# Activations copied by DMA and transposed through their float32r view, SSD and forget rows in other queues and buffers

## The chip, the cores and the metric

One Trainium2 chip, one of its cores. The metric is the time of one execution on the device in microseconds (us); lower is better. Six units of the core appear below: TensorE (PE, with its weight loads PEld), VectorE (DVE), ScalarE (ACT), GpSimd (POOL), SyncE (SP) and the 16 DMA engines.

## The reference

Three transformer blocks follow each other on x, 256 tokens by 1024 features, in float32. Block one has two layers of feed-forward, mixer, feed-forward and a gated embedding; block two a hybrid mixer and an expert layer (PEER); block three a forgetting mixer and a convolutional feed-forward. What the change touches:

```python
def swiglu(x, w_in, w_out):                        # four times in block one; D_FF = 2816
    gate, up = jnp.split(x @ w_in, 2, axis=-1)
    return (jax.nn.silu(gate) * up) @ w_out

# PEER, 16384 experts, per token the gates gc of its chosen experts
act = jnp.einsum('td,thkd->thk', xc, u)
hact = jax.nn.gelu(act, approximate=False) * gc
return jnp.einsum('thk,thkd->td', hact, jnp.take(v_tab, ec, axis=0))

# SSD, 32 heads: a cumulative sum over time enters each head's decay matrix
acum = jnp.cumsum(ac, axis=1)
lmat = jnp.exp(jnp.where(causal, acum[:, :, None] - acum[:, None, :], -jnp.inf))

# forgetting attention, 16 heads, in blocks of 128 queries
sc = q @ k.T * scale + cum[:, :, qs:qe, None] - cum[:, :, None, :qe]
p = jax.nn.softmax(jnp.where(allowed, sc, -jnp.inf), axis=-1)
```

## The kernel before

**Products.** The tokens are two row tiles t of 128. Weights come as 900 chunks of 128x1024 float32 (`chunk`, L120 to L130): SP issues the DMA into one of 5 `raw` buffers, ACT copies it to a float32r high part `wh` (L128), DVE subtracts for the low part `wl` (L129), 8 buffers each. Every product is three float32r matmuls, high by high, low by high and high by low: L177, L178 and L181 in `seg`, L874 to L876 in the forms with other operands.

**Transposes.** An activation must lie with its features on the partitions before it can be multiplied. `split_T` (L217 to L228) transposes 128x128 blocks on PE against an identity `ident` (L225), up to four into one PSUM tile `tp`, of which there are two; ACT copies the high part out (L227), DVE computes the low part (L228).

**Feed-forward** (`ffn`, L343 to L372). The 2816 hidden columns are taken in five chunks of 512 and one of 256. For each chunk and each t, PE accumulates gate and up, ACT applies Silu (L364), DVE multiplies into `hnat` (L366), and `split_T` (L369) transposes four blocks (two in the last chunk). The next chunk's matmuls are already in PE's queue around these transposes.

**PEER** (`peer`, from L1481). The activations of all 16384 experts are computed densely and stored to DRAM (`act_d`, L1507), as are the gates (`gate_d`). Then 32 chunks of 512 experts follow: `prepare` (L1650) loads `va` (L1658) and `vg` (L1660) in SP's queue, DVE multiplies them in place (L1661), `split_T` (L1662) transposes `va`, and the chunk is multiplied with its weights.

**SSD and forget rows.** The cumulative sums are stored to DRAM (`cum_d`, L1256; in block three L1097) and read back repeated on all partitions by `rows_bcast` (L456 to L459), in SP's queue. In the SSD mixer, `unit(g)` (L1269) reads `RA` and `RB` (the tile `sil`) of group g; POOL masks them (L1295), ACT forms the exponentials (L1302, L1303) and Silu (L1291), PE multiplies (L1307, L1308, L1315). In block three `prep` (L1128 to L1133) loads `fR`, POOL masks it (L1132), DVE adds it to the scores (L1137); `attention` (L888 to L936) does scores (L885), softmax and the transposes into `apT` (L916, L922), for units of heads that `skew` (L41) runs interleaved. MoBA attention in block two uses the same function.

**Order.** Each engine executes its own queue in order. The order is fixed when the program is built, by a scheduler that places instructions by its estimates; a wait at the head of a queue holds all that stands behind it.

Of the kernel before, what the change touches and what calls it, by code (L numbers as in the profile page):

```python
# [16 lines left out]
P = 128  # L17
# [22 lines left out]

def skew(units):  # L41

    live = []
    units = list(units)
    while units or live:
        if units:
            live.insert(0, units.pop(0))
        live = [u for u in live if next(u, "end") != "end"]
        yield
# [13 lines left out]
class Net:  # L63
# [17 lines left out]
    def consts(self):  # L81
        nc = self.nc
        self.ident = self.cp.tile([P, P], F32, name="ident")
        nc.gpsimd.memset(self.ident, 0.0)
        nc.gpsimd.affine_select(out=self.ident, in_=self.ident, compare_op=ALU.not_equal, fill=1.0,
                                base=0, pattern=[[-1, P]], channel_multiplier=1)
        self.triu = self.cp.tile([P, P], F32, name="triu")
        nc.gpsimd.memset(self.triu, 1.0)
        nc.gpsimd.affine_select(out=self.triu, in_=self.triu, compare_op=ALU.is_ge, fill=0.0,
                                base=0, pattern=[[1, P]], channel_multiplier=-1)  # L90
        self.ones = self.cp.tile([P, P], F32, name="ones")
        nc.gpsimd.memset(self.ones, 1.0)
        self.cmask = self.cp.tile([P, P], F32, name="cmask")
        nc.gpsimd.memset(self.cmask, 0.0)
        nc.gpsimd.affine_select(out=self.cmask, in_=self.cmask, compare_op=ALU.is_ge, fill=NEG,
                                base=0, pattern=[[-1, P]], channel_multiplier=1)
        self.neghalf = self.cp.tile([P, 16], F32, name="neghalf")
        nc.gpsimd.memset(self.neghalf, -0.5)
# [117 lines left out]

    def split_T(self, src, dst_h, dst_l):  # L217

        nc = self.nc
        nb = src.shape[1] // P  # L220
        for b0 in range(0, nb, 4):
            m = min(4, nb - b0)
            tp = self.tp()
            for b in range(m):
                nc.tensor.transpose(tp[:, b * P:(b + 1) * P], src[:, (b0 + b) * P:(b0 + b + 1) * P], self.ident)  # L225
            v = tp[:, :m * P].rearrange("p (b t) -> p b t", t=P)
            nc.scalar.activation(dst_h[:, b0:b0 + m, :], v, AF.Copy)  # L227
            nc.vector.tensor_sub(dst_l[:, b0:b0 + m, :], v, dst_h[:, b0:b0 + m, :].bitcast(F32))  # L228
# [109 lines left out]
    def ffn(self, x, g_pre, g_post, l, i):  # L338
# [11 lines left out]
        for wd in widths:  # L350
# [11 lines left out]
            for t in range(2):  # L362
                sil = self.work("sil", [P, 512])
                nc.scalar.activation(sil[:, :wd], acc[t][:, :wd], AF.Silu, scale=rs[t])  # L364
                h = self.work("hnat", [P, 512])
                nc.vector.scalar_tensor_tensor(h[:, :wd], acc[t][:, wd:2 * wd], rs[t], sil[:, :wd],  # L366
                                               op0=ALU.mult, op1=ALU.mult)
                b0, nb = c0 // P, wd // P
                self.split_T(h[:, :wd], hs[t][:, b0:b0 + nb, :], ls[t][:, b0:b0 + nb, :])  # L369
            c0 += wd  # L370
# [84 lines left out]

    def rows_bcast(self, out, rows):  # L456

        (sa, na), (sb, nb) = rows.ap
        self.nc.sync.dma_start(out, bass.AP(tensor=rows.tensor, offset=rows.offset, ap=[[0, P], [sa, na], [sb, nb]]))  # L459

# [427 lines left out]
    def attention(self, mp, qT, kT, v, hs, ls, logits, prep=None):  # L888
# [3 lines left out]
        def unit(t, b0):  # L892
# [22 lines left out]
            yield  # L915
            pT = mp.tile([P, nb, 2, t + 1, P], F32, tag="apT", bufs=2, name=f"apT{u}")  # L916
            flat = pT.rearrange("p b j k q -> p (b j k) q")
# [17 lines left out]

        return skew(unit(t, b0) for t in range(2) for b0 in range(0, 8, 4 >> t))  # L936

# [125 lines left out]
    def forget_mixer(self, x):  # L1063
# [5 lines left out]
        with pool("spill3", space=bass.MemoryType.DRAM) as dp:  # L1069
# [6 lines left out]
            with pool("fgt") as fp:  # L1076
# [46 lines left out]
                with pool("fattn", reuse_waits="tile") as mp, pool("fyT", reuse_waits="tile") as yp:  # L1123
# [4 lines left out]
                    def prep(t, b0, W):  # L1128
                        R = mp.tile([P, W, (t + 1) * P], F32, tag="fR", bufs=1, name=f"fR{t}_{b0}")
                        self.rows_bcast(R, cumd[2 * b0:2 * b0 + W, :(t + 1) * P])  # L1130
# [37 lines left out]
            with pool("merge", reuse_waits="tile") as mp:  # L1168
                hs, ls, lhy = self.xT_tiles("yaT", 10, pool=mp)
                for t in range(2):  # L1170
                    for y, c in yn[t]:
                        k = slice(c // P, (c + y.shape[1]) // P)
                        self.split_T(y, hs[t][:, k, :], ls[t][:, k, :])
                merge(1, accb)
# [65 lines left out]
    def ssd(self, lhs, h_all, l_all, cumd, mp):  # L1240
# [14 lines left out]
        nc.vector.tensor_tensor_scan(lp, self.ones[:32, :1].to_broadcast([32, N]), a, 0.0, ALU.mult, ALU.add)  # L1255
        nc.sync.dma_start(cumd, lp)  # L1256
        nat = mp.tile([P, 4, 32], F32, name="dt_acum")
# [11 lines left out]
        def unit(g):  # L1269
# [4 lines left out]
            for R, c in ((RA, 0), (RB, P)):  # L1274
                self.rows_bcast(R, cumd[4 * g:4 * g + 4, c:])
            w = self.weights("w_in_2", (0,), kbs, [(OX + 256 * g, 256), (OX + 2048 + P * g, P), (OX + 3072 + P * g, P)])
# [204 lines left out]
    def peer(self, x):  # L1481
# [5 lines left out]
        with self.tc.tile_pool(name="peer_d", bufs=1, space=bass.MemoryType.DRAM) as dp:  # L1487
# [3 lines left out]
            with self.tc.tile_pool(name="peer1", bufs=1) as mp:  # L1491
# [156 lines left out]
                with self.tc.tile_pool(name="peer2", bufs=1) as vp:  # L1648
# [3 lines left out]
                    def prepare(c):  # L1652
# [3 lines left out]
                        for t in range(2):  # L1656
# [4 lines left out]
                            nc.vector.tensor_mul(a, a, gt)  # L1661
                            self.split_T(a, h[:, :, t * P:(t + 1) * P], l[:, :, t * P:(t + 1) * P])  # L1662
                        return [lambda kb, t=t: (h[:, kb, t * P:(t + 1) * P], l[:, kb, t * P:(t + 1) * P])
# [93 lines left out]
```

## Time and profile before

| | |
|---|---|
| time, median of 3 runs | 2857.23 us (2855.98 to 2858.57) |
| profiled execution: its own time | 2861.38 us |
| its span from first to last instruction | 2859.7 us |
| TensorE busy | 2797.2 us (98%) |
| VectorE, ScalarE, GpSimd busy | 1857.2, 1624.1, 115.9 us |
| DMA | 601.31 MB, 210 GB/s in the mean |

A row of the timeline joins equal instructions that follow each other (x4); its second number is from the first's start to the last's end. TensorE's matmuls overlap, so that the time of one is read from the distance of their starts. A bracket tells how long the engine was idle before the row, and what released it.

### The profile page before, as it was taken

The page shows a single profiled execution, that of the slowest core. Times are in us where ns is not written, and L with a number is a line of the kernel's source. Part 1 is how long each engine was busy: PE and PEld are TensorE (multiplying, and loading weights), DVE is VectorE, ACT ScalarE, POOL GpSimd, SP SyncE. Part 2 cuts the span into 40 slices and gives each one's busy share as a digit, 9 for nine tenths or more (in the row PEclk, how much of TensorE's full clock was granted, in tenths as well). Part 3 has the DMA queues.
Part 4 walks back from the last instruction along what each step waited for, and adds up shares of the span by engine and source line. Part 5 has one row for each costly group of instructions (what it writes and reads, how often), then busy time and mean ns, then how long its engine had stood idle before and what let it go on. Part 6 is the DMA issues. An engine that isn't in the chain of part 4 may idle for free. (4 is left out here: it accounts for less than half of the span.)

```text
span 2859.7 us, 39692 instructions
## 1 busy us (share of the span) xinstructions
PE 2797.2 (98%) x14844; PEld 2369.0 (83%) x14844; DVE 1857.2 (65%) x2641; ACT 1624.1 (57%) x2356; POOL 115.9 (4%) x178
## 2 busy tenths in 40 slices
PE   8999999999989999999999999999999999999998
PEld 7887788888768878999779878888888888877997
DVE  5555654755566466776664999566666657776784
ACT  5446544644475456777565469684444448655653
POOL 0000000200010012100000000000000000000000
PEclk9999999999999999999999999999999999999999
DMA  7554555665536465665656668788777756565553
GB/s 251 189 204 159 189 191 182 232 209 189 209 105 217 166 219 190 196 223 192 221 184 208 212 217 264 243 257 311 268 271 267 269 178 225 178 237 189 195 178 125
DMA packets 221161, 601.31 MB, mean 210 GB/s; under 512 B 21172, under 2 KB 67044, under 8 KB 220456
## 3 DMA queue, kind: packets, MB, share of 16 engines
q1 hardware_dynamic: 220664, 597.72, 61.8%
q8 instruction: 116, 1.90, 0.3%
q10 hardware_dynamic: 272, 1.05, 0.1%
q14 instruction: 77, 0.63, 0.1%
q0 software_dynamic: 32, 0.02, 0.0%
HBM read 548.84 MB, written 49.86 MB: 209 GB/s over the span
## 5 line engine op out<-in xcount | busy, mean ns | idle before, releaser
L129 DVE TENSOR_TENSOR wl<-raw,wh 128x1024 fp32r<-128x1024 f32 x900 | 1079.1, 1221 | 578.5 <-ACT wh L128 551.2
L128 ACT ACTIVATE wh<-raw 128x1024 fp32r<-128x1024 f32 x900 | 926.9, 1055 | 706.6 <-PE acc L181 522.9
L177 PE MATMUL acc<-wh,xTh_h 128*128 128x512 f32 (+2 forms) x1552 | 591.4, 383 | 0.8 <-ACT act L1506 0.5
L178 PE MATMUL acc<-wl,xTh_h 128*128 128x512 f32 (+2 forms) x1552 | 585.4, 379 | 2.6 <-DVE wl L129 2.6
L181 PE MATMUL acc<-wh,xTl_l 128*128 128x512 f32 (+2 forms) x1552 | 462.2, 379 | 0.0
L178 PEld LDWEIGHTS acc<-wl,xTh_h 128*128 128x128 f32 x1552 | 293.4, 189 | 53.7 <-DVE wl L129 2.9
L177 PEld LDWEIGHTS acc<-wh,xTh_h 128*128 128x128 f32 x1552 | 293.4, 189 | 53.1 <-issue 1.0
L181 PEld LDWEIGHTS acc<-wh,xTl_l 128*128 128x128 f32 x1552 | 286.2, 189 | 54.0 <-issue 1.0
L874 PE MATMUL acc<-xTh_h,wh 128*128 128x256 f32 x832 | 237.9, 286 | 0.5 <-DVE big L1395 0.5
L876 PE MATMUL acc<-xTh_h,wl 128*128 128x256 f32 x832 | 237.3, 285 | 0.0
L875 PE MATMUL acc<-xTl_l,wh 128*128 128x256 f32 x832 | 236.8, 285 | 0.0
L177 PE MATMUL acc<-wh,ehT 128*128 128x512 f32 x512 | 202.2, 395 | 0.4 <-ACT ehT L227 0.4
L178 PE MATMUL acc<-wl,ehT 128*128 128x512 f32 x512 | 199.5, 390 | 0.0
L874 PEld LDWEIGHTS acc<-xTh_h,wh 128*128 128x128 f32 x832 | 160.4, 193 | 0.9 <-ACT wh L128 0.7
L876 PEld LDWEIGHTS acc<-xTh_h,wl 128*128 128x128 f32 x832 | 160.5, 193 | 0.2
L875 PEld LDWEIGHTS acc<-xTl_l,wh 128*128 128x128 f32 x832 | 160.4, 193 | 0.2
L178 PE MATMUL acc<-wl,hTh_h 128*128 128x512 f32 x352 | 137.6, 391 | 0.0
L177 PE MATMUL acc<-wh,hTh_h 128*128 128x512 f32 x352 | 137.6, 391 | 0.0
L181 PE MATMUL acc<-wh,elT 128*128 128x512 f32 x512 | 137.0, 389 | 0.0
L204 POOL TENSOR_SCALAR s<-s 128x1 f32<-128x1 f32 (+3 forms) x66 | 30.6, 463 | 2287.0 <-ACT junk L214 2024.1
L181 PEld LDWEIGHTS acc<-wh,elT 128*128 128x128 f32 x512 | 96.1, 188 | 20.0
L177 PEld LDWEIGHTS acc<-wh,ehT 128*128 128x128 f32 x512 | 96.2, 188 | 19.5 <-ACT ehT L227 0.6
(483 smaller groups left out, 4203.9 us busy)
## 6 DMA issues: line engine op xcount, KB each, us to landing
raw<-in_w_dram SPq DMA_DIRECT2D x900, 512.0 KB, 4.8
act_d<-act SPq DMA_DIRECT2D x64, 256.0 KB, 3.6
gate_d<-gst SPq DMA_DIRECT2D x32, 512.0 KB, 5.0
va<-act_d SPq DMA_DIRECT2D x64, 256.0 KB, 5.2
vg<-gate_d SPq DMA_DIRECT2D x64, 256.0 KB, 5.1
gain<-in_norm_g_dram SPq DMA_DIRECT2D x18, 512.0 KB, 5.7
RA<-cum_d SPq DMA_DIRECT2D x8, 512.0 KB, 4.8
sg_d<-big SPq DMA_DIRECT2D x8, 512.0 KB, 5.8
```

What stands on the lines that cost most here:

```text
L128: nc.scalar.activation(hi, raw, AF.Copy)
L129: nc.vector.tensor_sub(lo, raw, hi.bitcast(F32))
L177: nc.tensor.matmul(o, xh, wh[:, s], start=first and i == 0, stop=False)
L178: nc.tensor.matmul(o, xh, wl[:, s], start=False, stop=False)
L181: nc.tensor.matmul(o, lhs[t](kbs[i])[1], w[i][0][:, s], start=False, stop=last and i == end)
L204: nc.gpsimd.tensor_scalar(m, ss, c / n, c * EPS, op0=ALU.mult, op1=ALU.add)
L874: nc.tensor.matmul(o, wh[:, s], xh, start=i == 0, stop=False)
L875: nc.tensor.matmul(o, wh[:, s], xl, start=False, stop=False)
L876: nc.tensor.matmul(o, wl[:, s], xh, start=False, stop=i == len(kbs) - 1)
```

## The change

An identity of type float32r, `identr`, takes the place of the float32 one, which becomes its view. A new function `loaded` copies an activation within on-chip memory by a DMA in GpSimd's queue, into one of two buffers, and `split_T` can transpose such a tile through float32r views of it, of the identity and of the PSUM tile. The feed-forward's `hnat` (48 copies, 176 transposes) and PEER's product (64 copies, 256 transposes) are copied and transposed so; the tiles `yn` of block three, which a DMA has loaded already, are transposed so without a copy (20 transposes). The other 658 transposes stay float32. In the SSD mixer the store of `cum_d` and the rows of group 0 go to GpSimd's queue. `fR` has two buffers instead of one, `apT` one instead of two, and the attention's units are advanced eldest first.

```diff
@@ -38,13 +38,14 @@
         return self.got[t]
 
 
-def skew(units):
+def skew(units, eldest=False):
+
 
     live = []
     units = list(units)
     while units or live:
         if units:
-            live.insert(0, units.pop(0))
+            live.insert(len(live) if eldest else 0, units.pop(0))
         live = [u for u in live if next(u, "end") != "end"]
         yield
 
@@ -80,11 +81,13 @@
 
     def consts(self):
         nc = self.nc
-        self.ident = self.cp.tile([P, P], F32, name="ident")
-        nc.gpsimd.memset(self.ident, 0.0)
-        nc.gpsimd.affine_select(out=self.ident, in_=self.ident, compare_op=ALU.not_equal, fill=1.0,
+        self.identr = self.cp.tile([P, P], F32R, name="identr")
+        self.ident = self.identr.bitcast(F32)
+        self.triu = self.cp.tile([P, P], F32, name="triu")
+        nc.gpsimd.memset(self.triu, 0.0)
+        nc.gpsimd.affine_select(out=self.triu, in_=self.triu, compare_op=ALU.not_equal, fill=1.0,
                                 base=0, pattern=[[-1, P]], channel_multiplier=1)
-        self.triu = self.cp.tile([P, P], F32, name="triu")
+        nc.scalar.activation(self.identr, self.triu, AF.Copy)
         nc.gpsimd.memset(self.triu, 1.0)
         nc.gpsimd.affine_select(out=self.triu, in_=self.triu, compare_op=ALU.is_ge, fill=0.0,
                                 base=0, pattern=[[1, P]], channel_multiplier=-1)
@@ -214,7 +217,14 @@
         nc.scalar.activation(junk[:, :n], src, AF.Square, scale=scale, accum_out=ss)
         return ss
 
-    def split_T(self, src, dst_h, dst_l):
+    def loaded(self, src, pool, tag, bufs=2):
+
+        self.n_small += 1
+        c = pool.tile(list(src.shape), F32, tag=tag, bufs=bufs, name=f"{tag}_{self.n_small}")
+        self.nc.gpsimd.dma_start(c, src)
+        return c
+
+    def split_T(self, src, dst_h, dst_l, loaded=False):
 
         nc = self.nc
         nb = src.shape[1] // P
@@ -222,7 +232,11 @@
             m = min(4, nb - b0)
             tp = self.tp()
             for b in range(m):
-                nc.tensor.transpose(tp[:, b * P:(b + 1) * P], src[:, (b0 + b) * P:(b0 + b + 1) * P], self.ident)
+                o, i = tp[:, b * P:(b + 1) * P], src[:, (b0 + b) * P:(b0 + b + 1) * P]
+                if loaded:
+                    nc.tensor.transpose(o.bitcast(F32R), i.bitcast(F32R), self.identr)
+                else:
+                    nc.tensor.transpose(o, i, self.ident)
             v = tp[:, :m * P].rearrange("p (b t) -> p b t", t=P)
             nc.scalar.activation(dst_h[:, b0:b0 + m, :], v, AF.Copy)
             nc.vector.tensor_sub(dst_l[:, b0:b0 + m, :], v, dst_h[:, b0:b0 + m, :].bitcast(F32))
@@ -366,7 +380,8 @@
                 nc.vector.scalar_tensor_tensor(h[:, :wd], acc[t][:, wd:2 * wd], rs[t], sil[:, :wd],
                                                op0=ALU.mult, op1=ALU.mult)
                 b0, nb = c0 // P, wd // P
-                self.split_T(h[:, :wd], hs[t][:, b0:b0 + nb, :], ls[t][:, b0:b0 + nb, :])
+                c = self.loaded(h[:, :wd], fp, f"hcopy{wd}")
+                self.split_T(c, hs[t][:, b0:b0 + nb, :], ls[t][:, b0:b0 + nb, :], True)
             c0 += wd
         acc = self.gemm_wide(hl, DFF // P, "w_ffn_out", (l, i))
         fctx.close()
@@ -453,10 +468,10 @@
 
         self.nc.tensor.transpose(out, col.to_broadcast([P, P]), self.ident)
 
-    def rows_bcast(self, out, rows):
+    def rows_bcast(self, out, rows, queue=None):
 
         (sa, na), (sb, nb) = rows.ap
-        self.nc.sync.dma_start(out, bass.AP(tensor=rows.tensor, offset=rows.offset, ap=[[0, P], [sa, na], [sb, nb]]))
+        (queue or self.nc.sync).dma_start(out, bass.AP(tensor=rows.tensor, offset=rows.offset, ap=[[0, P], [sa, na], [sb, nb]]))
 
     def transposes(self, dst, src, nb, engine="act"):
 
@@ -913,7 +928,7 @@
                 e = sm[:, c * half:(c + 1) * half, :]
                 nc.vector.tensor_mul(e, e, ri[:, c * half:(c + 1) * half, None].to_broadcast([P, half, nk]))
             yield
-            pT = mp.tile([P, nb, 2, t + 1, P], F32, tag="apT", bufs=2, name=f"apT{u}")
+            pT = mp.tile([P, nb, 2, t + 1, P], F32, tag="apT", bufs=1, name=f"apT{u}")
             flat = pT.rearrange("p b j k q -> p (b j k) q")
             for c in range(2):
                 tp = self.tp([P, 4, P])
@@ -933,7 +948,7 @@
             nc.scalar.activation(hs[t][:, b, :], o, AF.Copy)
             nc.vector.tensor_sub(ls[t][:, b, :], o, hs[t][:, b, :].bitcast(F32))
 
-        return skew(unit(t, b0) for t in range(2) for b0 in range(0, 8, 4 >> t))
+        return skew((unit(t, b0) for t in range(2) for b0 in range(0, 8, 4 >> t)), True)
 
     def rg_lru(self, lhs, ga, ya, mp):
 
@@ -1126,7 +1141,7 @@
                     hs, ls, lhy = self.xT_tiles("yT", KB, pool=yp)
 
                     def prep(t, b0, W):
-                        R = mp.tile([P, W, (t + 1) * P], F32, tag="fR", bufs=1, name=f"fR{t}_{b0}")
+                        R = mp.tile([P, W, (t + 1) * P], F32, tag="fR", bufs=2, name=f"fR{t}_{b0}")
                         self.rows_bcast(R, cumd[2 * b0:2 * b0 + W, :(t + 1) * P])
                         diag = R[:, :, t * P:]
                         nc.gpsimd.affine_select(out=diag, in_=diag, compare_op=ALU.is_ge, fill=-NEG, base=0,
@@ -1170,7 +1185,7 @@
                 for t in range(2):
                     for y, c in yn[t]:
                         k = slice(c // P, (c + y.shape[1]) // P)
-                        self.split_T(y, hs[t][:, k, :], ls[t][:, k, :])
+                        self.split_T(y, hs[t][:, k, :], ls[t][:, k, :], True)
                 merge(1, accb)
                 acca = self.gemm_wide(lhy, 10, "w_proj_a_3", (0,))
                 mh, ml, lhm = self.xT_tiles("mT", KB, pool=mp)
@@ -1253,7 +1268,7 @@
         nc.vector.scalar_tensor_tensor(f, f, 0.0, lp, op0=ALU.max, op1=ALU.add)
         nc.vector.tensor_scalar(a, f, ea, None, op0=ALU.mult)
         nc.vector.tensor_tensor_scan(lp, self.ones[:32, :1].to_broadcast([32, N]), a, 0.0, ALU.mult, ALU.add)
-        nc.sync.dma_start(cumd, lp)
+        nc.gpsimd.dma_start(cumd, lp)
         nat = mp.tile([P, 4, 32], F32, name="dt_acum")
         neg = mp.tile([P, 2, 32], F32, name="nacum")
         dt, acum, nacum = [nat[:, t, :] for t in range(2)], [nat[:, 2 + t, :] for t in range(2)], [neg[:, t, :] for t in range(2)]
@@ -1272,7 +1287,7 @@
             RB = self.work("sil", [P, 512]).rearrange("p (h t) -> p h t", h=4)
 
             for R, c in ((RA, 0), (RB, P)):
-                self.rows_bcast(R, cumd[4 * g:4 * g + 4, c:])
+                self.rows_bcast(R, cumd[4 * g:4 * g + 4, c:], None if g else nc.gpsimd)
             w = self.weights("w_in_2", (0,), kbs, [(OX + 256 * g, 256), (OX + 2048 + P * g, P), (OX + 3072 + P * g, P)])
             acc = self.acc2([P, 4, N])
             self.segT(lhs[2], kbs, w, [acc[:, n, :] for n in range(4)])
@@ -1659,7 +1674,8 @@
                             gt = vp.tile([P, 512], F32, tag="vg", bufs=4, name=f"vg{c}{t}")
                             nc.sync.dma_start(gt, gdv[t, :, e])
                             nc.vector.tensor_mul(a, a, gt)
-                            self.split_T(a, h[:, :, t * P:(t + 1) * P], l[:, :, t * P:(t + 1) * P])
+                            a = self.loaded(a, vp, "vc")
+                            self.split_T(a, h[:, :, t * P:(t + 1) * P], l[:, :, t * P:(t + 1) * P], True)
                         return [lambda kb, t=t: (h[:, kb, t * P:(t + 1) * P], l[:, kb, t * P:(t + 1) * P])
                                 for t in range(2)]
 
```

PE's queue at the border of two feed-forward chunks, before. `hnat_478` is t=0, `hnat_489` is t=1; `acc_37` belongs to the next chunk.

```order
L181 MATMUL acc_30_331<-wh_424,xTl_l_110 128x512 x2
L225 MATMUL tp_480<-ident,hnat_478 128x128 x4
L177 MATMUL acc_37_498<-wh_502,xTh_h_109 128x512
L178 MATMUL acc_37_498<-wl_503,xTh_h_109 128x512
L177 MATMUL acc_37_498<-wh_502,xTh_h_109 128x512
L178 MATMUL acc_37_498<-wl_503,xTh_h_109 128x512
L181 MATMUL acc_37_498<-wh_502,xTl_l_110 128x512 x2
L225 MATMUL tp_491<-ident,hnat_489 128x128 x4
L177 MATMUL acc_37_498<-wh_508,xTh_h_109 128x512
```

After, the same border; `hcopy_35` and `hcopy_39` are the copies for t=0 and t=1. First the transposes of t=0 and what follows them:

```order
L184 MATMUL acc_32_336<-wh_429,xTl_l_111 128x512 x2
L237 MATMUL tp_487<-identr,hcopy_35_485 128x128 x4
L180 MATMUL acc_41_507<-wh_511,xTh_h_110 128x512
L181 MATMUL acc_41_507<-wl_512,xTh_h_110 128x512
L180 MATMUL acc_41_507<-wh_511,xTh_h_110 128x512
L181 MATMUL acc_41_507<-wl_512,xTh_h_110 128x512
L184 MATMUL acc_41_507<-wh_511,xTl_l_111 128x512 x2
```

They are where they were. Six rows further on in PE's queue stands this, with the transposes of t=1 (`tp_500`):

```order
L181 MATMUL acc_41_507<-wl_524,xTh_h_110 128x512
L180 MATMUL acc_41_507<-wh_523,xTh_h_110 128x512
L181 MATMUL acc_41_507<-wl_524,xTh_h_110 128x512
L184 MATMUL acc_41_507<-wh_523,xTl_l_111 128x512 x2
L237 MATMUL tp_500<-identr,hcopy_39_498 128x128 x4
L180 MATMUL acc_41_507<-wh_529,xTh_h_110 128x512
L181 MATMUL acc_41_507<-wl_530,xTh_h_110 128x512
```

The transposes of t=0 stay at the border. Those of t=1 stood 6 matmuls behind them and now stand 18 behind, after the matmuls of three weight tiles (`wh_511`, `wh_517`, `wh_523`) instead of one.

SP's queue at the store of the SSD mixer's cumulative sum, before.

```order
L125 DMA raw_9144<-in_w_dram 128x1024
L1256 DMA cum_d<-hnat_8738 32x256
L459 DMA RA_8757<-cum_d 128x1024
L459 DMA sil_8758<-cum_d 128x4x128
L459 DMA RA_9128<-cum_d 128x1024
L459 DMA sil_9129<-cum_d 128x4x128
L125 DMA raw_9150<-in_w_dram 128x1024
L125 DMA raw_9270<-in_w_dram 128x1024
```

After, SP's queue at that place.

```order
L128 DMA raw_9235<-in_w_dram 128x1024
L128 DMA raw_9241<-in_w_dram 128x1024
L474 DMA RA_9225<-cum_d 128x1024
L128 DMA raw_9247<-in_w_dram 128x1024
L474 DMA sil_9226<-cum_d 128x4x128
L128 DMA raw_9367<-in_w_dram 128x1024
L128 DMA raw_9373<-in_w_dram 128x1024
```

The store and the first group's two rows are no longer there; the second group's stand between weights. GpSimd's queue at that place, after:

```order
L1271 DMA cum_d<-hnat_8835 32x256
L474 DMA RA_8854<-cum_d 128x1024
L474 DMA sil_8855<-cum_d 128x4x128
L1310 AFFINE_SELECT RA_9225<-RA_9225 128x4x128
L1310 AFFINE_SELECT RA_8854<-RA_8854 128x4x128
L1310 AFFINE_SELECT sil_8855<-sil_8855 128x512
L1310 AFFINE_SELECT sil_9226<-sil_9226 128x512
```

The store and the rows of the first group (`RA_8854`, `sil_8855`) stand here now, ahead of the masks.

SP's queue in the forgetting attention, before.

```order
L125 DMA raw_22313<-in_w_dram 128x1024
L459 DMA fR_0_21771<-cum_d 128x8x128
L1060 DMA sg_d<-big_21814 128x2x512
L125 DMA raw_22319<-in_w_dram 128x1024
L125 DMA raw_22325<-in_w_dram 128x1024
L125 DMA raw_22417<-in_w_dram 128x1024
L1119 DMA sil_22519<-ya_d 128x256
L459 DMA fR_4_21864<-cum_d 128x8x128
```

The two loads of `fR` are six rows apart. The same place, after:

```order
L128 DMA raw_22538<-in_w_dram 128x1024
L474 DMA fR_0_21996<-cum_d 128x8x128
L474 DMA fR_4_22102<-cum_d 128x8x128
L1075 DMA sg_d<-big_22039 128x2x512
L128 DMA raw_22544<-in_w_dram 128x1024
L128 DMA raw_22550<-in_w_dram 128x1024
L128 DMA raw_22642<-in_w_dram 128x1024
L474 DMA fR_0_22243<-cum_d 128x1024
```

The second load of `fR` now stands directly behind the first.

## Rows read from the trace of the kernel before

**Rows 1.** The page's first part: busy us (share) and instructions of each engine.
```profile
PE 2797.2 (98%) x14844; PEld 2369.0 (83%) x14844; DVE 1857.2 (65%) x2641; ACT 1624.1 (57%) x2356; POOL 115.9 (4%) x178
```

**Rows 2.** Waits of PE, whole span: line, releaser, total us, times, longest us.
```profile
PE tp L1315 <- ACT big L1404: 5.9, 2, 3.8
...
PE acc L1307 <- ACT ssdu L1291: 2.1, 1, 2.1
...
PE tp L225 <- DVE hnat L366: 1.3, 1, 1.3
```

**Rows 3.** Timeline at a feed-forward border: start, us, engine, line, operation [idle before].
```profile
77.85 0.75 DVE L366 SCALAR_TENSOR_TENSOR hnat<-acc,s,sil 128x512 f32<-128x512 f32 x1 [3.84 <-ACT sil L364]
...
82.37 0.60 PE L225 MATMUL tp<-ident,hnat 128*128 128x128 f32 x4
...
83.44 0.74 DVE L366 SCALAR_TENSOR_TENSOR hnat<-acc,s,sil 128x512 f32<-128x512 f32 x1
...
84.25 0.66 PE L225 MATMUL tp<-ident,hnat 128*128 128x128 f32 x4
```

**Rows 4.** Windows: PE, PEld, DVE, ACT, POOL busy, PEclk, DMA share, GB/s.
```profile
78.00:79.00 1.00, 1.00 (x6) 0.81 (x6) 0.60 (x1) 0.51 (x1) 0.00 (x0) 1.00 0.00 0
84.00:89.00 5.00, 5.00 (x25) 4.04 (x24) 2.55 (x4) 1.29 (x2) 0.00 (x0) 1.00 0.86 300
1138.00:1143.00 5.00, 5.00 (x31) 5.00 (x32) 2.38 (x3) 5.00 (x12) 3.10 (x2) 0.68 0.28 108
1960.00:2320.00 360.00, 359.65 (x1717) 300.36 (x1715) 223.33 (x246) 153.37 (x186) 0.00 (x0) 1.00 0.77 264
2520.00:2525.00 5.00, 5.00 (x19) 3.52 (x16) 3.55 (x4) 3.34 (x7) 0.98 (x1) 0.66 0.77 234
```

**Rows 5.** Source view of L225: engine, tiles, count, ns min/median/max, first and last start.
```profile
L225 PE MATMUL tp<-ident,va x256: 270/272/273, 1959.7 to 2315.3; 128*128 128x128 f32 x128
...
L225 PE MATMUL tp<-ident,hnat x176: 270/272/331, 35.4 to 986.5; 128*128 128x128 f32 x176
```

**Rows 6.** Timeline in the PEER stage at 1959 us.
```profile
1959.74 1.03 PE L225 MATMUL tp<-ident,va 128*128 128x128 f32 x8
```

**Rows 7.** Timeline of PE from 1142 to 1146 us.
```profile
1142.02 0.28 PE L876 MATMUL acc<-xTh_h,wl 128*128 128x256 f32 x1
...
1145.98 0.28 PE L876 MATMUL acc<-xTh_h,wl 128*128 128x256 f32 x1
```

**Rows 8.** Timeline in the PEER stage, 2013 to 2034 us.
```profile
2013.84 1.07 PE L181 MATMUL acc<-wh,elT 128*128 128x512 f32 x4
...
2014.79 0.69 DVE L1661 TENSOR_TENSOR va<-va,vg 128x512 f32<-128x512 f32 x1 [0.89 <-DMA va<-act_d]
...
2031.96 1.03 PE L225 MATMUL tp<-ident,va 128*128 128x128 f32 x8
```

**Rows 9.** Timeline around GpSimd's `cum_d` in the third block.
```profile
2372.38 0.68 DVE L1096 TENSOR_TENSOR_SCAN hnat<-ones,hnat 16x256 f32<-16x256 f32 x1
...
2373.36 0.71 POOL L1097 DMA_DIRECT2D cum_d<-hnat  x1 [28.91 <-DVE hnat L1096]
```

**Rows 10.** DMA view, 2370 to 2376 us: issues, KB each, median us to landing.
```profile
cum_d<-hnat POOLq DMA_DIRECT2D x1, 16.0 KB, 1.9
```

**Rows 11.** The page's sixth part: DMA issues, KB each, median us to landing.
```profile
act_d<-act SPq DMA_DIRECT2D x64, 256.0 KB, 3.6
```

**Rows 12.** Timeline around the SSD rows, SP's queue and ACT.
```profile
1118.30 3.13 SPq L125 DMA_DIRECT2D raw<-in_w_dram  x4
...
1126.23 1.06 ACT L128 ACTIVATE wh<-raw 128x1024 fp32r<-128x1024 f32 x1 [6.78 <-DMA raw<-in_w_dram]
```

**Rows 13.** Waits from 2495 to 2575 us.
```profile
POOL fR L1132 <- DMA fR<-cum_d: 26.1, 4, 7.4
...
DVE asm L1137 <- POOL fR L1132: 9.2, 6, 4.9
...
PE acc L885 <- DVE asm L1137: 3.4, 2, 2.1
```

## The prediction

> **What bounds the kernel now.** I read the page first: TensorE is busy 2797.2 of 2859.7 us, 98% [rows 1]. So only two things can move the time: how long TensorE's own instructions are, and the few places where it waits. The list of what TensorE waits for comes second; its waits are small and each stands at one place: 5.9 us in the SSD mixer (two waits for ScalarE's `big`, L1404), 2.1 us there for `ssdu` (L1291), and 1.3 us in one wait for `hnat` [rows 2]. The third view is the timeline where the change adds a wait, at the border of two column chunks of a feed-forward layer [rows 3]. The fourth is a table of windows, because the new copies go through the same DMA engines as the weights: these engines stand still at 78 to 79 us and are 86% busy from 84 to 89 us [rows 4].
>
> **The float32r view of 452 transposes.** 44 transposes in each of four feed-forward layers (176), 256 in PEER and 20 of `yn` in the third block change their type; 176 and 256 are the counts of the rows of L225 [rows 5]. Matmuls are pipelined, so their median of 272 ns is not what one costs. Eight transposes in one row take 1.03 us; without the last one's 0.27 that is 0.76 over seven steps, 0.109 us each [rows 6]. A float32r instruction with 128 columns is not in this trace. Those with 256 columns follow each other every 0.12 us (from 1142.02 to 1145.98, 33 steps) [rows 7], and those with 512 every 0.227 (four in 1.07 us, the last 0.39 of it: 0.68 / 3) [rows 8]. The straight line through both is 0.107 us for 256 columns and 0.013 besides, so 0.066 for 128. That is the low end. The high end is 0.120, if 128 columns cost what 256 do. I take 0.075, near the line, a little above it because the weights of a transpose are loaded for it alone and nothing wider hides that. 452 × (0.109 − 0.075) = **−15.4 us**; ends −19.4 and +5. It counts in full, since TensorE has no slack in these stages: from 1960 to 2320 us it is busy 359.65 of 360 us [rows 4].
>
> **The 48 feed-forward copies.** Before, TensorE transposes what VectorE has just written. At this border the second half (t=1) is ready at 83.44 + 0.74 = 84.18 and transposed from 84.25: a slack of 0.07 us. The first half (t=0) is ready at 77.85 + 0.75 = 78.60 and transposed at 82.37: 3.77 us [rows 3]. Now a copy by DMA stands between. The new order gives the t=1 transposes 12 more float32r matmuls of 0.227 us before them (11 in the first and the last chunk of a layer), while the t=0 transposes ahead of them are 4 × 0.034 us shorter: 0.07 + 12 × 0.227 − 0.14 = 2.65, or 2.43 with 11. Sixteen and eight of these make a mean slack of 2.57 us, in 24 places.
>
> How long is it from `hnat` to the landed copy? The nearest row is the only transfer that GpSimd issues after a VectorE result: the scan ends at 2372.38 + 0.68 = 2373.06, GpSimd issues at 2373.36 (0.30 later), and its 16 KB land 1.9 us after issue [rows 9, 10]. The copy is 256 KB, about 245 KB more. From 1960 to 2320 us the engines move 264 GB/s at a share of 0.77, so 343 at full share [rows 4]: 0.72 us more alone, 1.43 at half rate beside weights. So 0.30 + 1.9 + 0.72 = 2.9 us or 3.6. The t=0 copy falls into the stretch without DMA traffic [rows 4], and 2.9 us are covered by 3.77 us of matmuls. The t=1 copy, from 84.5 us on, falls into weight traffic at a share of 0.86: 0.86 × 1.43 + 0.14 × 0.72 = 1.33, so 3.5 us. The same 256 KB in SP's queue, `act_d`, take 3.6 us from issue [rows 11], but some of that is weights ahead of them in that queue, and a part of the 1.9 is already the transfer of the 16 KB. I take 3.4 us. TensorE then waits 3.4 − 2.57 = 0.83 us 24 times, as nothing else can run ahead of the transposes in its queue: **+20 us**. Ends: 2.9 us gives +8, 3.6 us +25; without end at the bottom a copy in 2.57 us gives 0.
>
> The Trainium skill ("DMA: Bandwidth & Descriptors", section "Anatomy of one DMA — SWDGE (gpsimd) path") puts a transfer of this kind at about 2.0 us and its bytes over 436 GB/s, 2.6 us here as an estimate; with the sum otherwise as it stands, this term would be about +1 in place of +20. The same page ("Queues, rings and completion order") says that each DMA engine takes turns between queues packet by packet, which speaks for half the rate beside weights. No transfer of 256 KB by GpSimd is in this trace, so neither is shown.
>
> **The 64 PEER copies.** The product of a chunk is done at 2014.79 + 0.69 = 2015.48 and its transposes start at 2031.96 [rows 8]: 16.5 us for a copy of 3.5. Two `vc` buffers allow a copy to start only when the chunk before is transposed, about 11 us ahead (356 us for 32 chunks [rows 5]); that still covers it. They add 16.8 MB to a stage whose DMA share is 0.77 [rows 4]; 16.8 MB over 360 us are 47 GB/s, a share of 0.14 more, so 0.91. **0**; if weights then come late I would expect +5.
>
> **SSD rows in other queues.** SP issues `cum_d` and four loads of its rows (1.5 MB) before the next weights, which it issues at 1118.30. ScalarE is idle 6.78 us, until 1126.23, for these weights [rows 12]. This delay comes back to TensorE as the 2.1 and 5.9 us of L1307 and L1315 [rows 2], and behind the second wait the granted clock is 0.68 of full from 1138 to 1143 (a part of these 5 us at 1.2 GHz, the rest at 2.4) [rows 4], 1.6 us lost. Now half of the rows stand in GpSimd's queue, and SP goes on with weights. Their bytes still share the engines, so half of the 6.78 us is saved at best: **−3 us**; ends 0 and −9.6, all three.
>
> **Forget rows, two buffers.** With one `fR`, the next load waits until the masked scores are read; GpSimd waits 26.1 us for these loads and TensorE 3.4 us in two pieces for what follows [rows 13], with 0.66 clock from 2520 to 2525 (1.7 us lost) [rows 4]. Now two loads stand back to back in SP's queue. −3.5 of the possible −5.1; on the other side, one `apT` instead of two and the order that begins with the eldest unit may cost 2: ends −5.1 and +2. The MoBA attention uses the same order; I give it 0 (±2), and the start, where `identr` takes one more ScalarE step, 0.
>
> **Sum.** −15.4 + 20 − 3 − 3.5 = −1.9 on the profiled execution's 2861.38: 2859.5. That execution is 4.15 above the median of 2857.23, so by the median **2855 us**. Without the copies' term the sum is −21.9, so the whole question is the landing time: at 3.48 us the change is worth nothing; under 3.24 it is faster by over 0.2% (5.7 us, about what a measurement of this kernel can tell from no change), over 3.72 slower by as much.
>
> **The rivals.** *The copies land in time.* If a landing takes 2.6 us, the t=1 term is 24 × 0.03, and the sum is −21: 2836. For it: the 1.9 us row is a write to DRAM of small packets, and a copy within SBUF may be quicker. Against it: 0.30 and 1.9 alone are 2.2, and 245 KB must pass in 0.4 us, at over 600 GB/s, more than any window here moves. The skill's 2.6 us gives the same time.
>
> *The copies are later than I think.* If weights go first at each engine and the copy gets a third of the rate, its transfer is 2.15 us and the landing 4.35: a wait of 1.78 × 24 = 43, sum +21, 2878. It decides from 3.72 us on. The granted clock fell behind the longest wait of the forget rows, 2.1 us [rows 4, 13]; should it fall behind these waits, they cost more. For it: `act_d`'s 3.6 us [rows 11]. Against it: at 84 to 89 us the engines have a seventh of their time free.
>
> *The view gains nothing.* If a 128-column transpose keeps its 0.109 us in either type, only +20 − 6.5 is left: 2871. For it: 256-column instructions take 0.12, so a floor per instruction can't be excluded. Against it: f32 transposes take twice what the line gives. The Trainium skill ("TensorE: Matmul & The Clock Gate", section "Terms") says that the transpose mode of this chip is four times faster for FP32; by that rule the f32 transposes are in the fast form already and this rival holds.
>
> **How the numbers follow.** Forecast, late by 0.3 to 1.2 us: 0.45, its own range 2841 to 2866; within it about 0.17 faster, 0.18 same, 0.10 slower. In time: 0.28, all faster. Later: 0.15, all slower. No gain: 0.12, of which 0.02 still within the bound. Together 0.45 faster, 0.20 same, 0.35 slower. The range runs from 2830 (in time with 0.066 us a transpose is 2832; only larger gains at the SSD and forget rows lie lower) to 2879 (the third-rate case).
>
> **What would show it.** The float32r transposes of `vc` in steps of 0.075 us (0.066 to 0.109): eight in about 0.8 us. TensorE's wait for DMA `hcopy` at t=1, 24 times, some 20 us in all; none at t=0; the DMA list's landing of `hcopy512` about 3.1 us from issue. The waits of L1307, L1315 and the scores' matmuls together some 6 us shorter. The prediction fails if t=0 copies are waited for too, if PEER's transposes wait for `vc`, or if weights come late in the PEER stage.

## The result: 2.6% slower

The changed kernel takes 2934.4 us (median of 4 runs, 2927.7 to 2935.4) against 2856.9 for the kernel before: a ratio of 1.0264, 95% interval 1.0252 to 1.0277. The forecast of 2855 was wrong, and so was its range. The profiled execution of the changed kernel took 2935.37 us, with a span of 2933.6.

The page of the changed kernel, part one, and two of its DMA issues (KB each, median us to landing), answer to [rows 1, 11]:

```profile
PE 2816.5 (96%) x14844; PEld 2375.3 (81%) x14844; DVE 1853.3 (63%) x2641; ACT 1624.4 (55%) x2357; POOL 178.4 (6%) x293
...
vc<-va POOLq DMA_DIRECT2D x64, 256.0 KB, 3.9
hcopy<-hnat POOLq DMA_DIRECT2D x40, 256.0 KB, 3.3
```

TensorE has as many instructions as before, is busy 19 us longer and idle 55 us longer. Its waits (total us, times, longest), beside [rows 2, 13]:

```profile
PE tp L237 <- DMA hcopy<-hnat: 56.9, 24, 3.6
...
PE tp L1330 <- ACT big L1419: 4.2, 2, 2.9
PE tp L237 <- DMA vc<-va: 2.8, 1, 2.8
...
PE acc L900 <- DVE asm L1152: 1.7, 1, 1.7
...
PE acc L1322 <- ACT ssdu L1306: 0.3, 1, 0.3
```

One new wait accounts for nearly all of the added idle time. It stands 24 times, as the prediction said, but lasts 2.37 us and not 0.83. The waits of L1307, L1315 and L885 (now L1322, L1330 and L900) are together 6.2 us instead of 11.4: 5.2 less, where the prediction had some 6.

The four feed-forward layers, from the same TensorE instruction to the same one, in windows (PE, PEld, DVE, ACT, POOL busy; granted clock; DMA share; GB/s). First of the kernel before, then of the changed kernel:

```profile
8.30:188.40 180.10, 178.28 (x800) 146.60 (x801) 99.99 (x97) 88.28 (x99) 0.97 (x3) 1.00 0.61 210
337.80:492.30 154.50, 154.47 (x702) 126.97 (x701) 82.87 (x81) 71.84 (x80) 0.00 (x0) 1.00 0.56 190
601.30:755.70 154.40, 154.40 (x701) 127.00 (x701) 81.84 (x80) 70.90 (x79) 0.00 (x0) 1.00 0.57 196
866.60:1020.20 153.60, 153.60 (x703) 126.44 (x701) 78.85 (x78) 70.33 (x80) 0.22 (x1) 1.00 0.55 188
sum 642.60, PE 640.75 PEld 527.01 DVE 343.55 ACT 301.35 POOL 1.18; mean PE 160.19 PEld 131.75 DVE 85.89 ACT 75.34 POOL 0.30
```

```profile
7.90:207.10 199.20, 183.66 (x801) 149.21 (x802) 100.43 (x97) 88.27 (x99) 8.84 (x17) 0.97 0.59 206
356.40:531.80 175.40, 160.54 (x702) 130.89 (x701) 83.48 (x81) 71.99 (x81) 5.90 (x11) 0.96 0.53 182
640.80:815.00 174.20, 160.87 (x702) 130.91 (x701) 82.54 (x80) 70.85 (x79) 5.90 (x11) 0.96 0.55 187
925.30:1101.30 176.00, 161.70 (x703) 131.52 (x702) 79.32 (x78) 70.35 (x80) 6.76 (x13) 0.95 0.52 180
sum 724.80, PE 666.78 PEld 542.52 DVE 345.76 ACT 301.47 POOL 27.41; mean PE 166.69 PEld 135.63 DVE 86.44 ACT 75.37 POOL 6.85
```

They take 724.8 us instead of 642.6: 82.2 us more, and the whole span grew by 73.9. 56.2 of them are idle time (58.0 against 1.85). The other 26 are busy time, because the granted clock, 1.00 in all four windows before, is 0.95 to 0.97: (1 − clock) times the length is 29 us, and the faster transposes take 3 to 4 off that. The 29 us do not come from every border: by the records of the granted clock, 16 of the 24 waits are followed by a stretch at half the clock, 58 us in all, and eight are not. A wait of 2.5 us and the clock behind it, in three windows of the changed kernel:

```profile
60.00:69.50 9.50, 7.47 (x36) 5.82 (x34) 6.11 (x6) 4.25 (x5) 0.55 (x1) 1.00 0.77 263
69.50:76.30 6.80, 6.30 (x18) 5.07 (x19) 0.69 (x1) 0.89 (x2) 0.00 (x0) 0.50 0.06 23
76.30:85.00 8.70, 8.70 (x40) 7.21 (x39) 4.90 (x4) 3.96 (x4) 0.00 (x0) 1.00 0.55 180
```

The wait ends at 70.0. From 69.5 to 76.3 the granted clock is 0.50, the lower of the two levels (1.2 GHz): 18 matmuls in 6.30 busy us are 0.35 us each, the 40 in the next 8.70 are 0.22.

Now the border itself, which answers to [rows 3]. Timeline of the changed kernel; 87.51 is the copy for t=0, 93.10 that for t=1:

```profile
87.51 0.55 POOL L224 DMA_DIRECT2D hcopy<-hnat  x1 [22.03 <-DVE hnat L380]
...
90.98 0.46 PE L237 MATMUL tp<-identr,hcopy 128*128 128x128 f32 x4
...
92.06 0.75 DVE L380 SCALAR_TENSOR_TENSOR hnat<-acc,s,sil 128x512 f32<-128x512 f32 x1
...
93.10 0.55 POOL L224 DMA_DIRECT2D hcopy<-hnat  x1 [5.04 <-DVE hnat L380]
...
98.16 0.51 PE L237 MATMUL tp<-identr,hcopy 128*128 128x128 f32 x4 [2.55 <-DMA hcopy<-hnat]
```

`hnat` is ready at 92.81, GpSimd issues 0.29 us later, and TensorE would have been ready at 95.61: a slack of 2.8 us at this border, 2.65 by the prediction (over the 24 borders 2.77, where it had 2.57). What failed is the landing. The DMA view, from 87 to 91 us (the t=0 copy) and from 92 to 99 us (the t=1 copy):

```profile
hcopy<-hnat POOLq DMA_DIRECT2D x1, 256.0 KB, 2.2
```

```profile
hcopy<-hnat POOLq DMA_DIRECT2D x1, 256.0 KB, 4.9
```

The same copy of 256 KB takes 2.2 us on idle DMA engines and 4.9 beside weights. Over the 24 borders, four of which have copies of 128 KB, the first is 1.9 to 2.5, the second 4.1 to 5.4 us (mean 4.7). The DMA view in two windows after the t=1 issue, 93.1 to 95.4 and 95.4 to 97.8 us (queue: packets, MB, share of 16 engines; q1 is the weights, q0 the copy), shows how:

```profile
q1 hardware_dynamic: 196, 0.74, 86.7%
```

```profile
q1 hardware_dynamic: 171, 0.59, 63.3%
q0 software_dynamic: 80, 0.26, 26.9%
```

For 2.3 us no packet of the copy moves; then its 80 packets take 2.2 us, among packets of weights. Alone, at t=0, the first packet moves 1.1 us after issue and all of them within 0.9.

### The profile page after: what moved, and what is told of

It is laid out like the page before. It is cut to its first block, busy times and chain, and to the rows that moved or that the text cites. A ratio compares the mean times of both kernels' runs of the same rounds, so it can differ in the third digit from the quotient of the medians.

```text
span 2933.6 us, 40143 instructions
## 1 busy us (share of the span) xinstructions
PE 2816.5 (96%) x14844; PEld 2375.3 (81%) x14844; DVE 1853.3 (63%) x2641; ACT 1624.4 (55%) x2357; POOL 178.4 (6%) x293
## 4 chain that ended last, share of the span: by engine, by line
PE 66%; issue 16%; DVE 7%; DMA 5%; ACT 4%; POOL 2%; SPq 0%; DVEq 0%; POOLq 0%; ACTq 0%
PE acc L180 14%; PE acc L184 14%; PE acc L181 14%; PE acc L891 3%; PE acc L890 3%; PE acc L889 3%; DVE wl L132 2%; PE acc L342 2%; DMA hcopy<-hnat 2%; PE acc L343 2%; DMA raw<-in_w_dram 2%; PE acc L345 2%; ACT wh L131 1%; PE acc L1612 1%; PE tp L237 1%
## 5 line engine op out<-in xcount | busy, mean ns | idle before, releaser
L180 PE MATMUL acc<-wh,xTh_h 128*128 128x512 f32 (+2 forms) x1552 | 601.3, 390 | 0.8 <-ACT act L1521 0.5
L181 PE MATMUL acc<-wl,xTh_h 128*128 128x512 f32 (+2 forms) x1552 | 594.2, 385 | 2.5 <-DVE wl L132 2.5
L184 PE MATMUL acc<-wh,xTl_l 128*128 128x512 f32 (+2 forms) x1552 | 472.2, 386 | 0.0
L180 PEld LDWEIGHTS acc<-wh,xTh_h 128*128 128x128 f32 x1552 | 299.5, 193 | 55.8 <-issue 2.0
L181 PEld LDWEIGHTS acc<-wl,xTh_h 128*128 128x128 f32 x1552 | 299.5, 193 | 55.4 <-DVE wl L132 2.9
L1676 DVE TENSOR_TENSOR va<-va,vg 128x512 f32<-128x512 f32 x64 | 43.3, 692 | 139.2 <-DMA va<-act_d 128.1
L181 PEld LDWEIGHTS acc<-wl,ehT 128*128 128x128 f32 x512 | 96.8, 189 | 19.4
```

The source lines that it names most:

```text
L180: nc.tensor.matmul(o, xh, wh[:, s], start=first and i == 0, stop=False)
L181: nc.tensor.matmul(o, xh, wl[:, s], start=False, stop=False)
L184: nc.tensor.matmul(o, lhs[t](kbs[i])[1], w[i][0][:, s], start=False, stop=last and i == end)
```

## The experiments

Theory A: the loss is the t=1 copies, which stand behind weight packets on the DMA engines. Rivals: other edits lose too (B), the copies cost by their traffic (C), or GpSimd's path is slow at t=1 for another reason (D).

**Without the feed-forward copies** (`no_ffn_copy`).

```diff
-                c = self.loaded(h[:, :wd], fp, f"hcopy{wd}")
-                self.split_T(c, hs[t][:, b0:b0 + nb, :], ls[t][:, b0:b0 + nb, :], True)
+                self.split_T(h[:, :wd], hs[t][:, b0:b0 + nb, :], ls[t][:, b0:b0 + nb, :])
```

> The changed kernel without the 48 feed-forward copies (their 176 transposes are float32 again, straight from the product); all other edits stay. Theory A: the loss is made by the late t=1 copies alone (57 us of waits for them, some 26 us of low clock behind these waits, less 4 us that the faster transposes give), so without them 2934 falls by about 80 to 2851 us (2846 to 2856). Rival B: the float32r transposes, the PEER copies or the moved rows lose too; then the time stays above 2865 us.

2856.9 us against 2856.5 for the kernel before, ratio 1.0001 (0.9991 to 1.0010). The whole loss of 77.5 us is gone; B is out. But the time is above the expected band (2846 to 2856): the remaining edits together gain nothing that can be measured, not 5 us.

**The feed-forward copies alone** (`ffn_copies_only`): the kernel before with `loaded` in the feed-forward and nothing else of the change.

> The kernel before with the 48 feed-forward copies and their 176 float32r transposes, nothing else of the change. Theory A: the whole loss is here, 24 waits of about 2.4 us and the low clock behind them: 2934 us (2928 to 2940). If the copies lose only together with the other edits: under 2900 us.

2939.7 us in one run, with 56.3 us of waits in 24 places. The loss is complete without any other edit.

**A quiet DMA** (`quiet_weights`).

```diff
+        if not again:                       # again: w_ffn_in, three of four chunks
+            self.raw = self.wp.tile([P, CH], F32, tag="raw", bufs=RAWB, name=f"raw{i}")
+            nc.sync.dma_start(self.raw, self.d["w"][i])
+        raw = self.raw
```

> The changed kernel, but only one of four weight chunks of the feed-forward's first matrix is loaded and used four times (a quarter of the weights is multiplied, three quarters are left out); all instructions of TensorE, ScalarE and VectorE and all copies stay. Theory A (the t=1 copies queue with weight traffic on the DMA engines): their landing falls from 4.7 to about 2.3 us after issue, as at t=0, and the 57 us of waits fall under 12 us: about 2865 us. Rival D (GpSimd's path is slow at t=1 for another reason, VectorE's work for example): landing stays near 4.7 us and the time near 2930 us.

2878.4 us in one run. Waits of PE and DMA issues of this kernel:

```profile
PE tp L239 <- DMA hcopy<-hnat: 17.9, 8, 2.8
```

```profile
hcopy<-hnat POOLq DMA_DIRECT2D x40, 256.0 KB, 2.3
```

16 of the 24 waits are gone: there the t=1 copies land 2.25 to 2.32 us after issue, as at t=0, with the same work on VectorE and ScalarE. The 8 waits that are left are the last two borders of each layer, where the next matrix, which is loaded in full, passes; there the landing is still 4.0 to 5.2 us. The time is 13 us above my 2865: 6 us are waiting beyond the 12 that I had allowed, and the kernel without feed-forward copies, too, takes 6 us more than I had expected of it. The traffic decides, border by border: A holds, D falls.

**Another queue** (`copies_act_queue`): `nc.scalar.dma_start` in place of GpSimd's.

> The changed kernel with the feed-forward copies issued from ScalarE's queue instead of GpSimd's. Theory A (queueing with weight packets on the DMA engines): the t=1 landing stays 1.5 us or more above the t=0 landing, waits stay above 35 us and the time stays above 2900 us. Rival D (GpSimd's own path is what is slow at t=1): the t=1 landing falls to the t=0 one, near 2 us, and the time to about 2865 us.

2929.6 us in one run. Waits of PE, and the DMA view from 60 to 66 us (t=0) and from 116 to 123 us (t=1):

```profile
PE tp L237 <- DMA hcopy<-hnat: 54.7, 24, 3.5
```

```profile
hcopy<-hnat ACTq DMA_DIRECT2D x1, 256.0 KB, 2.3
```

```profile
hcopy<-hnat ACTq DMA_DIRECT2D x1, 256.0 KB, 4.8
```

The same two landings from a queue that GpSimd has no part in. Which engine issues the copy makes no difference that this run can tell: its time lies within those of the changed kernel.

**Later transposes** (`late_split`): the copies stay for the 512-wide chunks, their transposes are emitted in the middle of the next chunk; the 256-wide chunks are not copied.

```diff
+                    if half:
+                        flush()             # split_T of the chunk before, from its copies
                     self.seg(lhs, kbs, w, ...
...
+                    due.append((self.loaded(h, fp, "hcopy512"),) + o)
```

> The changed kernel with all copies of the 512-wide chunks, but their transposes are placed behind the first half of the next chunk, about 48 matmuls (11 us) after the border, in place of 0 and 18; the 256-wide last chunk of each layer is not copied. Theory A: copies that land 5 us after issue are no longer waited for; the time is that of the kernel without feed-forward copies less 160 x 0.023 us: about 2847 us (2842 to 2853). Rival C: the copies cost also by their traffic (weights come later) or by GpSimd's issue: above 2855 us.

2853.0 us, ratio 0.9992 (0.9982 to 1.0001), no wait for `hcopy` at all. That is 81 us below the changed kernel with 40 of its 48 copies still made: feed-forward copies that nobody waits for cost nothing that can be measured, and C is out there. Against the kernel without feed-forward copies it is 3.9 us less, near the expected 3.7, but the difference of the two medians is uncertain by about as much.

**The view without copies** (`f32r_no_copy`): VectorE's product is written as float32r and transposed at once. The rounding leaves out the low part of these activations, so this kernel is less exact.

```diff
-                h = self.work("hnat", [P, 512])
+                h = fp.tile([P, 512], F32R, tag="hnatr", bufs=2, name=f"hnatr{c0}_{t}")
...
+                            nc.vector.tensor_mul(ar, a, gt)      # ar is F32R, in PEER
```

> No copies at all: VectorE writes the feed-forward and the PEER product as float32r, and the same transposes read that; SSD, forget and yn edits stay. The low part of these activations is left out by the rounding; every instruction of TensorE is as in the changed kernel. What the view is worth by itself, with copies at no cost: 452 x 0.023 = 10 us by the steps of the changed kernel's trace. Theory A: 5 us below the kernel without feed-forward copies for the 176 transposes and 5 more for the first PEER chunks, which no longer wait for a copy: about 2841 us (2836 to 2847). If the view gains nothing: 2851 us.

2842.3 us, ratio 0.9952 (0.9935 to 0.9968): 14.6 us below the kernel without feed-forward copies, in which PEER's copies remain.

**The SSD queues alone** (`ssd_queues_only`) and **the forget edits alone** (`forget_edits_only`), each put into the kernel before.

> The kernel before with the SSD edits alone: the store of cum_d and the rows of group 0 in GpSimd's queue. In the changed kernel's trace the stretch around these rows is 6 us shorter than before, 5 us in the kernel without feed-forward copies. If that is this edit: 2851.5 us (2849 to 2854). Rival: what is gained there is not in the timed runs, as the kernel without feed-forward copies was no faster than before: 2856 us.

2853.0 us against 2856.8, ratio 0.9988 (0.9978 to 0.9997): a gain of 3.8 us, within the band of the first case (2849 to 2854).

> The kernel before with two fR buffers, one apT buffer and the attention's units eldest first, nothing else. In the traces the forgetting attention is 8 to 9 us shorter than before, and a little later, and at the end of the MoBA attention too, 2.4 us are lost, 4 us gained in all: 2852.5 us (2850 to 2855). If the eldest-first order gives back all of it: 2856 us.

2857.5 us, ratio 1.0000 (0.9991 to 1.0010): nothing. In its trace, by the distance between the same TensorE instructions, the forgetting attention is some 5 us shorter and the MoBA attention 2.5 us longer than in the profile of before; but that profile lies 4 us above its own median. The traces of all 13 kernels tell more. Measured against that profile, the forgetting attention is 3.8 to 6.5 us shorter in the ten kernels with its edits and 0 to 2.6 us in the three without. MoBA is 1.7 to 3.3 us longer in the seven with the new order and 0 to 2.4 us in the six with the old one. By the means, about 4 us are gained in one place and 1.5 lost in the other. The timed runs don't show the difference; their interval leaves room for a gain of 2.6 us. The single `apT` and the order were not tried apart, so which of the two lengthens MoBA stays open.

**Combinations.** `best_exact` is the late split, without copies for the first two PEER chunks and with the old MoBA order; `best_no_copy` is the view without copies with the old MoBA order; `best_rounded` adds seven norms written as float32r.

> All products as exact as in the changed kernel: the late split of the feed-forward (transposes 48 matmuls behind the border), no copy for the first two PEER chunks, the MoBA attention in its old order with two apT buffers. From 2853 us of the late split: less 5.7 us that the first PEER copies cost at the start of that stage, less 2.5 us that the MoBA attention lost by the new order: 2845 us (2840 to 2850).

2847.7 us, ratio 0.9962 (0.9949 to 0.9974); faster than both kernels, without rounding any activation. Whether the PEER copies that it keeps are always free is less sure. Its profiled execution, the slowest of six (2855.2), is 9 us longer in the later PEER chunks than that of the late split. From 2150 to 2300 us weights come late there, and TensorE waits in seven places:

```profile
ACT wh L131 <- DMA raw<-in_w_dram: 76.0, 39, 3.9
...
PE tp L237 <- DVE elT L242: 5.6, 7, 1.1
```

The other traces with these copies that were compared (the changed kernel, those without feed-forward copies, with the late split, with ScalarE's queue and with quiet weights) have no such waits there, and why they came in this execution is open.

> No copies, VectorE writes the feed-forward and the PEER product as float32r (their low part is left out by the rounding; the norms stay float32), SSD, forget and yn edits as in the change, the MoBA attention in its old order with two apT buffers. From 2842.3 us of the same kernel with the new MoBA order less the 2.5 us that this order lost: 2840 us (2837 to 2843).

2841.7 us, ratio 0.9944 (0.9931 to 0.9958). The MoBA order made no difference that can be told from the 2842.3 with the new one.

> No copies: VectorE writes the feed-forward and PEER products as float32r, and the scaled rows of seven of the norms too (112 more transposes in the float32r form; the low part of these activations is left out); MoBA in its old order. From 2842.3 us of the kernel without copies: less 2.5 us (MoBA) and 112 x 0.023 = 2.6 us: 2837 us (2833 to 2842).

2837.9 us, ratio 0.9929 (0.9912 to 0.9945), but with less exact activations in front of seven layers, the four feed-forwards of block one among them: its result is off by a relative 0.029.

## Why the prediction was wrong, point by point

**The landing of the t=1 copies: the step that failed.** I took 3.4 us from `hnat` to the landed copy and bounded it by 2.9 and 3.6 (4.35 in the rival). It is 0.3 + 4.7, about 5.0. I took the fixed part from a transfer that [rows 9, 10] show, and let only the bytes beyond it share the engines with the weights. The windows show that the part before the first packet is doubled too, 2.3 instead of 1.1 us (1.7 to 2.6 over the 24 borders). Bytes matter less than I thought: the 128 KB copies of the 256-wide chunks land 4.1 to 4.5 us after issue. I also read the row that warned of this, `act_d` with 3.6 us, away as a matter of its queue; the copy in a queue of its own took longer still. The Trainium skill's sum ("DMA: Bandwidth & Descriptors", "Anatomy of one DMA — SWDGE (gpsimd) path"), an estimate of 2.6 us for these bytes, is near the 2.2 us of the idle engines and says nothing of loaded ones. Like the 2.2 it counts from the issue, so the prediction, which put it in place of the whole way from `hnat`, left out the 0.30 us before the issue: its +1 should have read +8, and its rival of copies in time lost that support. The Trainium skill's rule of turns by whole packets ("Queues, rings and completion order") agrees with the 2.2 us in which packets of both kinds move. Why only weights move for 2.3 us before that, no run here shows.

**The price of a wait.** The place, the count (24) and the slack (2.65 against 2.8 us) were right, and t=0 was covered. The clock was missing: I named it as a condition, without a number. 56.9 us of waits brought 29 us of lost clock, half as much again. With 5.0 us for the landing and this factor the same sum would have read 24 × 2.43 × 1.5 − 21.9, some 66 us slower; with the gains that were measured (9, 3.8 and 0, below) it reads 75, against 77.5. The rival "later than I think" had the mechanism, but stopped at 2878.

**The float32r view.** Right in kind. Two rows of the changed kernel's timeline, and two of before:

```profile
2160.32 0.80 PE L237 MATMUL tp<-identr,vc 128*128 128x128 f32 x8
...
2195.16 0.80 PE L237 MATMUL tp<-identr,vc 128*128 128x128 f32 x8
```

```profile
1984.87 1.03 PE L225 MATMUL tp<-ident,va 128*128 128x128 f32 x8
...
1996.64 1.03 PE L225 MATMUL tp<-ident,va 128*128 128x128 f32 x8
```

Eight transposes take 0.80 us instead of 1.03; the last one's 0.25 off, a step is 0.079 us, where I had 0.075. A chunk is (2195.16 − 2160.32) / 3 = 11.61 us instead of 11.77: 0.16 us for eight, 0.020 each. The steps alone would give more, but the matmul that follows starts 0.09 us behind the last transpose instead of 0.03. 452 × 0.020 is 9 us, not 15.4. My argument for the view was also worded too strongly: 0.109 is 1.65 times the 0.066 of the line, not twice. The rival of no gain falls, and with it the reading of the Trainium skill's line on the transpose mode ("TensorE: Matmul & The Clock Gate", "Terms") that float32 transposes are as fast as they can be.

**PEER.** 0 was nearly right, by two errors that cancel: the steady chunks gain 5 us, and the first chunks lose as much, because there the transposes follow the product closely and wait for `vc` (2.8 us, and the low clock behind it). This was one of the signs that I had named against the prediction.

**SSD and forget rows.** −3 for SSD, −3.8 measured. −3.5 for the forget edits, 0 measured: the traces show a gain of about 4 us in its place, and I gave MoBA, which the same edit reorders and lengthens, nothing.

## What to carry to other kernels

A transfer put into a chain of work costs its landing time under the traffic of that moment, not that of an idle machine. Read the DMA share at the moment at which it will be issued; here a share of 0.86 doubled a landing of 2.2 us, with the wait for the first packet doubled as well as the transfer. Count such waits of TensorE, here 2.4 us each, with the low clock that followed two in three of them and cost half of the waits again. And place the consumer by the loaded landing: 48 matmuls behind the border instead of 18 made the same copies free, and writing the type that the transpose wants made them needless, at the price of the activations' low part.

## What was unexpected of the hardware

The two landings hardly depend on the queue: 2.2 and 4.9 us from GpSimd, 2.3 and 4.8 from ScalarE. And of a loaded landing nearly half, 2.2 of 4.7 us in the mean, is spent before the first packet moves.
